# Second attention of a two-layer trunk: part of the output projection made within the last heads' steps, the gate multiplied into its weights

## The chip, the cores and the metric

The kernel runs on one core of one Trainium2 chip. The metric is the device time of one execution in microseconds (us); lower is better. Engines are named as in the profile: PE (TensorE matmul), PEld (its weight loads), DVE (VectorE), ACT (ScalarE), POOL (GpSimd), SP (SyncE); a q behind a name is that engine's queue of transfers.

## The reference

Two layers over 512 latent tokens of 1024 features with 256 context tokens, all in float32. Each layer is a token mixer, a layer norm of the gated sum, and a gated feed-forward with a convolution. The change lies in layer 1, between its mixer (neighbourhood attention) and its feed-forward:

```
y, yc = na_mixer(a_lat, a_ctx, na_w_qkv[slot], na_rpb[slot], na_w_o[slot], need_ctx)
...
h_lat = layer_norm(DEEPNORM_ALPHA * h_lat + g1 * y, ln1_g[i], ln1_b[i])
f = conv_ffn(modulate(h_lat, sh2, sc2), ffn_w_in[i], ffn_conv_w[i], ffn_conv_b[i], ffn_w_out[i])
```

Here `y` is the attention's output `o` (512 tokens by 16 heads of 64) times `w_o` (1024 by 1024), and `g1` is a vector of 1024, one value for each output feature. So `g1 * (o @ w_o)` equals `o @ (w_o * g1)`.

## The kernel before

Every float32 product is three matmuls: each operand is split into a high part (`wh`, `oh`, `axh`: a CAST on ACT) and a low part (`wl`, `ol`, `axl`: raw minus high, on DVE or POOL), and `mm3` (line 132) adds high times high, low times high and high times low in one PSUM bank. Weights come as units of 128 by 2048 (`unit`, line 114): a transfer into one of two `raw` buffers, ACT casts, POOL or DVE subtractions. `unit` can multiply a gate into `raw` first (lines 117 to 119); before, only the last feed-forward's `w_out` did.

Layer 1's attention goes by 32 steps, one for each head and each half of the queries (lines 1156 to 1187). A step makes the scores (`scn`), maxima and exponentials (`sn`, `en`), the reciprocal (DVE, line 1076) and the scaling of `en` (POOL, line 1077), then, for the step before, transposes (`trn`, split into `pt` by ACT and DVE), the product with the values (`pvn`), and its sum into `on` (`otn` on ACT and DVE, then POOL, line 1111). `ORDER1` writes down in which places of a step these come and where extra work (`f0` to `f5`) goes in: other heads' projections, weight units (`n_unit`), and splits of finished parts of `on` (`n_part`). A scheduler of the framework then sets each engine's final order; each engine takes its own instructions strictly in that order.

The output projection has four tiles of 128 tokens. For each, eight chunks `c` of 128 features (two heads each) are multiplied with `w_o` into two banks `yps` of 512 columns: `out_mm` (line 148), six matmuls of 128x512 per chunk and tile, 192 in all. Chunks 0 to 6 of tile 0 and 0 to 3 of tile 1 can be made while the last step is still under way (lines 1171 to 1174); all others follow in `mixer_out` (line 756), which runs after the attention. It loads `xr`, the residual, on ACT's queue into two buffers (line 773; line 748 in the profile), multiplies it by `eg` (DVE, line 775) and adds `eb` (POOL by halves, line 693). When a tile's banks are full, DVE multiplies them by the gate (line 787), adds `xr` (line 792), takes the norm (lines 676 to 686, with `rs` on POOL, line 681); PE transposes `z` (`ltr`, line 703), ACT scales and casts (`ft`, `axh`), POOL or DVE makes `axl` (line 719). `u` (line 814) are the first matmuls of the feed-forward; for its first two units they take 256 tokens at a time, so that they need two tiles.

Of the kernel before, what the change touches and what calls it, by code (L numbers as in the profile page):

```python
# [16 lines left out]
D = 1024  # L17
# [27 lines left out]
def trunk(ctx, tc, x, cx, cc, ada_w, ada_b, vec, ln1_g, ln1_b, ln2_g, ln2_b, w_in, w_out, m_in, m_qb,  # L45
# [44 lines left out]
    sil = const.tile([128, KD, 32], F32, name="sil")  # L90
    nc.vector.memset(sil, 0.0)
    nc.scalar.activation(sil[:, :, 0:2], cct, AF.Silu)
# [44 lines left out]
    def wide(src, xw, eng):  # L137
        raw = load(src)
        nc.scalar.copy(xw[0], raw)
        eng.tensor_tensor(xw[1], raw, f(xw[0]), op=ALU.subtract)  # L140
        return xw
# [6 lines left out]
    def out_mm(pss, part, us, c):  # L148
        wh, wl = us[c // 2]
        for hf in range(2):  # L150
            b = (c % 2) * 1024 + hf * 512
            mm3(pss[hf], *part, wh[:, b:b + 512], wl[:, b:b + 512], c == 0, c == 7)

# [58 lines left out]
    # =================== layer 0: latent attention ===================  # L212
# [58 lines left out]
    # Features come by blocks. Two tiles of tokens keep up with them; of the others a first part of the sum over the  # L271
    # features, up to the block named here, is made between blocks and kept.
# [269 lines left out]
    # what fills in at a step of layer 0's attention (head of a group of four, group of queries), in places 0 to 2  # L542
# [45 lines left out]
    # layer 0's output weights and the first heads' output, split in pieces between the last steps  # L588
# [4 lines left out]
    def late_pieces():  # L593
# [5 lines left out]
        for u in range(4):  # L599
# [9 lines left out]
            if u == 2:  # L609
                # the buffers of the queries that no further head needs  # L610
# [114 lines left out]
    def new_a(slot):  # L725
        # the latent part in two halves of 256 tokens, but whole where its tokens are permuted (slot 1)
# [13 lines left out]
    def by_block(eng, dram_rows, t, sb, store):  # L740
        # rows of a tile of two grid rows lie in DRAM by (block of 8 columns, row, column)
# [14 lines left out]
    def mixer_out(layer, slot, o, w_o, nt, wl=None, us=(), done=(), banks=()):  # L756
# [7 lines left out]
        g1 = [bcast(wl, gates[layer, 0, s:s + 1], f"g1{s}") for s in range(2 if nt > 4 else 1)]  # L764
        e1 = affine(wp, ln2_g[0:1], ln2_b[0:1]) if layer else None
        dst = new_a(slot)
        for t in range(nt):
# [34 lines left out]
    def ffn(layer, a_in, nt, out_slot, groups):  # L802
# [8 lines left out]
        def up(c):  # L811
# [27 lines left out]
            if layer == 0:  # L839
                # latent tokens of a tile of two grid rows go by blocks of 8 columns: (block, row, column)  # L840
# [107 lines left out]
    # =================== layer 1: neighbourhood attention ===================  # L948
# [11 lines left out]
    us, parts, ends = [], {0: [], 1: []}, []  # L960

    def n_unit(u):
        if u < 12:
            nw[u] = unit(n_qkv[u], eng="m" if u < 2 else "p")
        elif u < 15:
            us.append(unit(n_o[u - 12]))
        else:
            us.append(wide(n_o[3], [acp.tile([128, KD * C], F32R, name="ac" + i, tag="ac" + i, bufs=1) for i in "hl"],
                           nc.gpsimd))

    def n_part(t, c0, c1):
        p, tag = (vp, "vn") if c1 <= 4 else (vp, "qs")
        hl = [p.tile([128, 4, 128], F32R, name=tag, tag=tag, bufs=13 if tag == "vn" else 2)[:, :c1 - c0]
              for i in range(2)]
# [126 lines left out]
    def n_out(h, jj):  # L1101
# [7 lines left out]
        for j in range(2):  # L1109
# [6 lines left out]
    # what fills in at a step of layer 1's attention (head of a group of four, half of the queries), in places 0 to 5  # L1116
# [7 lines left out]
             (3, 1): [[], [("bias", 4)], [("v", 3)], [], [], []]}  # L1124

# [28 lines left out]
    for n, cur in enumerate(steps + [None]):  # L1154
        prev = steps[n - 1] if n else None
        fl = [[] for _ in range(6)]
        if cur:
            h, jj = cur
            fl = fills1(h, jj)
            if (h, jj) == (14, 0):  # L1160
                fl[5].append(lambda: n_part(0, 0, 4))
            if (h, jj) == (14, 1):
                fl[5].append(lambda: n_unit(15))
            if (h, jj) == (15, 0):
                fl[5].append(lambda: n_part(0, 4, 7))
                fl[5].append(lambda: n_part(1, 0, 4))
        else:
# [4 lines left out]
            fl[3] += [lambda t=t, c=c: out_mm(pss[t], parts[t][c], us, c) for t, c0, c1 in ((0, 4, 7), (1, 0, 4))  # L1172
# [25 lines left out]
def layout(i):  # L1198
# [39 lines left out]
    us = []  # L1238
# [48 lines left out]
```

## Time and profile before

| | |
|---|---|
| median of 3 runs | 1791.41 us (1791.40 to 1794.37) |
| the profiled execution, as timed | 1791.4 us |
| its span in the trace | 1790.0 us |
| PE busy | 1714.9 us, 96% of the span, 9776 instructions |
| DVE, ACT, POOL busy | 1094.7, 820.9, 841.8 us |
| last `pvn` of the attention | starts 1356.63, takes 0.74 us |
| first `u` of the feed-forward | 1403.18 us |

Times in the trace count from the start of the span. A busy share is an average over stages; what a stage waits for stands in the waits of its engines, and a wait is put down to the instruction that ended it.

### The profile page before, as it was taken

Reading aid. Unit: us, or ns where it says so; the run is one execution under the profiler, and the core shown is the slowest. Engines: PE = TensorE matmul, PEld = TensorE weight load, DVE = VectorE, ACT = ScalarE, POOL = GpSimd, SP = SyncE. Lnnn points to the kernel's source line nnn. Section 1 sums busy time; section 2 is a strip of 40 time slices with the busy share of each in tenths; the row PEclk is TensorE's granted clock in tenths of the full one; section 3 lists DMA queues with packets and bytes.
Section 4 is the critical chain, followed back from the end, with each engine's and each line's share of the span. In section 5 each row is a group of like instructions: output and inputs, shape, how many; then the busy total and the mean of one; then the engine's idle time right before and its main releaser. Section 6 shows DMA issues by size and latency. Waiting matters only on the chain. (4 is left out here: it accounts for less than half of the span.)

```text
span 1790.0 us, 25828 instructions
## 1 busy us (share of the span) xinstructions
PE 1714.9 (96%) x9776; PEld 1463.1 (82%) x9776; DVE 1094.7 (61%) x1971; ACT 820.9 (46%) x1660; POOL 841.8 (47%) x808
## 2 busy tenths in 40 slices
PE   6999999998999999999999989999988899999996
PEld 4877878887888888888888878989977788888885
DVE  4477787775763555555457756766765634444587
ACT  2366666664554233233222266666672553333332
POOL 3224233433452233333227468768783644453464
PEclk8999999999999999999999999999999999999998
DMA  8324354334341222221122212111122432132231
GB/s 309 121 106 177 143 184 171 138 139 138 113 174 48 71 71 71 71 71 51 68 71 71 95 66 91 57 54 57 57 86 82 165 112 100 71 118 94 88 113 59
DMA packets 35845, 185.37 MB, mean 104 GB/s; under 512 B 4072, under 2 KB 6520, under 8 KB 19080
## 3 DMA queue, kind: packets, MB, share of 16 engines
q1 hardware_dynamic: 32552, 173.23, 27.4%
q10 hardware_dynamic: 3168, 10.49, 1.7%
q8 instruction: 77, 1.26, 0.3%
q14 instruction: 48, 0.39, 0.1%
HBM read 174.23 MB, written 9.50 MB: 103 GB/s over the span
## 5 line engine op out<-in xcount | busy, mean ns | idle before, releaser
L129 POOL TENSOR_TENSOR wl<-raw,wh 128x512 fp32r<-128x512 f32 x284 | 381.0, 1374 | 457.3 <-ACT wh L125 457.1
L133 PE MATMUL u<-axh,wh 128*128 128x512 f32 (+1 forms) x736 | 281.6, 383 | 4.4 <-DVE z L787 3.3
L125 ACT CAST wh<-raw 128x512 fp32r<-128x512 f32 x324 | 179.2, 621 | 232.5 <-PE u L134 103.5
L134 PE MATMUL u<-axl,wh 128*128 128x512 f32 (+1 forms) x736 | 281.1, 382 | 0.6 <-POOL axl L719 0.6
L135 PE MATMUL u<-axh,wl 128*128 128x512 f32 (+1 forms) x736 | 281.0, 382 | 0.0
L898 DVE TENSOR_TENSOR acc<-ops,acc 128x512 f32<-128x512 f32 x168 | 114.7, 688 | 175.5 <-PE ops L135 174.9
L133 PE MATMUL ops<-wh,hh 128*128 128x512 f32 x440 | 174.2, 396 | 10.8 <-DVE ut L836 7.0
L134 PE MATMUL ops<-wl,hh 128*128 128x512 f32 x440 | 174.3, 397 | 0.0
L135 PE MATMUL ops<-wh,hl 128*128 128x512 f32 x440 | 172.4, 395 | 0.0
L133 PEld LDWEIGHTS u<-axh,wh 128*128 128x128 f32 x736 | 139.7, 190 | 30.7 <-DVE z L787 3.5
L134 PEld LDWEIGHTS u<-axl,wh 128*128 128x128 f32 x736 | 139.7, 190 | 26.8 <-POOL axl L719 0.9
L135 PEld LDWEIGHTS u<-axh,wl 128*128 128x128 f32 x736 | 139.6, 190 | 26.5
L493 POOL TENSOR_SCALAR e<-e,st 128x768 f32<-128x768 f32 (+1 forms) x96 | 75.1, 783 | 167.8 <-DVE st L492 143.1
L832 ACT ACTIVATE ut<-u,vt 128x512 f32<-128x512 f32 x88 | 68.3, 777 | 185.2 <-DVE ut L836 86.1
L834 DVE SCALAR_TENSOR_TENSOR ut<-u,vt,ut 128x511 f32<-128x511 f32 x88 | 65.7, 746 | 128.3 <-ACT ut L832 128.3
L133 PEld LDWEIGHTS ops<-wh,hh 128*128 128x128 f32 x440 | 83.8, 191 | 28.5 <-issue 7.4
L135 PE MATMUL uc<-ach,wl 128*128 128x256 f32 x352 | 99.6, 283 | 0.0
L134 PE MATMUL uc<-acl,wh 128*128 128x256 f32 x352 | 99.6, 283 | 0.0
L133 PE MATMUL uc<-ach,wh 128*128 128x256 f32 x352 | 99.6, 283 | 0.0
L135 PEld LDWEIGHTS ops<-wh,hl 128*128 128x128 f32 x440 | 83.5, 190 | 18.0
L134 PEld LDWEIGHTS ops<-wl,hh 128*128 128x128 f32 x440 | 83.8, 190 | 15.3
L511 DVE TENSOR_TENSOR pl<-ptr,ph 128x512 fp32r<-128x512 f32 x112 | 76.3, 687 | 19.8 <-ACT ph L507 18.3
(480 smaller groups left out, 4367.9 us busy)
## 6 DMA issues: line engine op xcount, KB each, us to landing
raw<-w_in SPq DMA_DIRECT2D x44, 1024.0 KB
raw<-ada_w SPq DMA_DIRECT2D x40, 1024.0 KB
raw<-w_out SPq DMA_DIRECT2D x22, 1024.0 KB
raw<-n_qkv SPq DMA_DIRECT2D x12, 1024.0 KB
rr<-resid ACTq DMA_DIRECT2D x10, 512.0 KB
raw<-ada SPq DMA_DIRECT2D x4, 1024.0 KB
ar<-ada SPq DMA_DIRECT2D x8, 512.0 KB
raw<-m_o SPq DMA_DIRECT2D x4, 1024.0 KB
```

The lines of the kernel that those rows point to most:

```text
L125: nc.scalar.copy(hi[:, a:b], raw[:, a:b])
L129: e.tensor_tensor(lo[:, a:b], raw[:, a:b], f(hi[:, a:b]), op=ALU.subtract)
L133: nc.tensor.matmul(ps, ah, bh, start=start, stop=False)
L134: nc.tensor.matmul(ps, ah, bl, start=False, stop=False)
L135: nc.tensor.matmul(ps, al, bh, start=False, stop=stop)
L493: done["p"] = nc.gpsimd.tensor_scalar(e[:, :n], e[:, :n], st[:, 2:3], 1.0, op0=ALU.mult, op1=ALU.mult).ins
L511: nc.vector.tensor_tensor(pl, tr, f(ph), op=ALU.subtract)
L832: nc.scalar.activation(u, p, AF.Identity, bias=cb[:, i:i + 1], scale=cw[:, 3 * i + 1:3 * i + 2])
L834: nc.vector.scalar_tensor_tensor(u[:, 1:], p[:, :n - 1], cw[:, 3 * i:3 * i + 1], u[:, 1:], op0=ALU.mult, op1=ALU.add)
L898: nc.vector.tensor_tensor(a[:, sl], ps, a[:, sl], op=ALU.add)
```

## The change

1. `n_half` makes chunks 0 to 3 (heads 0 to 7) of tiles 1, 2 and 3 in a bank of its own, `yp`: 12 matmuls for each of three tiles and two halves, 72 in all. ACT copies the bank to `zp` in SBUF. A table, `LAST1`, puts these and the splits they need into the steps of heads 13 to 15.
2. In `mixer_out` POOL adds `zp` to `xr` for these tiles (six instructions of 128x512). The banks then take only chunks 4 to 7 of tiles 1 to 3; those of tile 1, but for the last, are made in the last step.
3. The gate is multiplied into the four units of `w_o` on DVE (four instructions of 128x512 each), and its vector is loaded at the start of layer 1. The eight multiplies of the banks (line 787) go; `z` is `xr` plus the bank.
4. For room, `sil` goes to another pool and the scratch space of the framework's dynamic transfers is set to 512.

```diff
-    def wide(src, xw, eng):
+    def wide(src, xw, eng, gate=None):
         raw = load(src)
+        for a in range(0, 2048 if gate is not None else 0, 512):
+            nc.vector.tensor_tensor(raw[:, a:a + 512], raw[:, a:a + 512], gate[:, a % D:a % D + 512], op=ALU.mult)
...
-    def out_mm(pss, part, us, c):
+    def out_mm(pss, part, us, c, first=0, stop=7, halves=(0, 1)):
         wh, wl = us[c // 2]
-        for hf in range(2):
+        for hf in halves:
             b = (c % 2) * 1024 + hf * 512
-            mm3(pss[hf], *part, wh[:, b:b + 512], wl[:, b:b + 512], c == 0, c == 7)
+            mm3(pss[hf], *part, wh[:, b:b + 512], wl[:, b:b + 512], c == first, c == stop)
...
                 by_halves(nc.gpsimd, xt, xt, e1[1], ALU.add)
+                if firsts[t]:
+                    by_halves(nc.gpsimd, xt, xt, zp[:, t - 1], ALU.add)
...
             for hf in range(2):
                 hs = slice(hf * 512, hf * 512 + 512)
                 ps = pss[hf]
-                nc.vector.tensor_tensor(z[:, hs], ps, g1[s][:, hs], op=ALU.mult)
                 if layer == 0:
+                    nc.vector.tensor_tensor(z[:, hs], ps, g1[s][:, hs], op=ALU.mult)
...
                 else:
-                    nc.vector.tensor_tensor(z[:, hs], xt[:, hs], z[:, hs], op=ALU.add)
+                    nc.vector.tensor_tensor(z[:, hs], xt[:, hs], ps, op=ALU.add)
...
+    g1t = bcast(p5, gates[1, 0, 0:1], "g1t")
+    zp = p5.tile([128, 3, D], F32, name="zp")
...
-            us.append(unit(n_o[u - 12]))
+            us.append(unit(n_o[u - 12], gate=g1t))
...
+    def n_half(t, hf):
+        ps = bank("yp", [128, 512])
+        for c in range(4):
+            out_mm([ps, ps], parts[t][c], us, c, 0, 3, (hf,))
+        nc.scalar.copy(zp[:, t - 1, hf * 512:hf * 512 + 512], ps)
...
+    LAST1 = {(13, 0): [(5, "part", (1, 0, 4))],
+             (13, 1): [(1, "half", (1, 0)), (4, "half", (1, 1)), (5, "part", (2, 0, 4))],
+             (14, 0): [(1, "half", (2, 0)), (5, "part", (3, 0, 4))],
+             (14, 1): [(1, "half", (2, 1)), (5, "unit", (15,))],
+             (15, 0): [(1, "half", (3, 0)), (5, "part", (0, 0, 4)), (5, "part", (0, 4, 7, "qs"))],
+             (15, 1): [(1, "half", (3, 1)), (5, "part", (1, 4, 7))]}
...
-            fl[3] += [lambda t=t, c=c: out_mm(pss[t], parts[t][c], us, c) for t, c0, c1 in ((0, 4, 7), (1, 0, 4))
+            fl[3] += [lambda t=t, c=c: out_mm(pss[t], parts[t][c], us, c, 4 * t) for t, c0, c1 in ((0, 4, 7), (1, 4, 7))
                       for c in range(c0, c1)]
...
-        a4 = mixer_out(1, 2, o, n_o, 4, wl, us, [7, 4], pss)
+        a4 = mixer_out(1, 2, o, n_o, 4, wl, us, [7, 7, 4, 4], pss, (0, 4, 4, 4), zp)
```

How this moves instructions is told by each engine's order, in which the new file's lines are some 2 to 12 higher. First DVE in the attention, where the third unit of `w_o` comes in. Line 1076 is the reciprocal before (1088 now), line 986 (998) the split of a value tile, and ISA the maximum with the bias. Before:

```order
L986 TENSOR_TENSOR vn<-vps,vn 128x4x64
L1063 TENSOR_REDUCE sn<-scn 128x1
L1076 RECIPROCAL sn<-sn 128x1
L1064 ISA scn,sn<-scn,bm_12935,sn 128x256
L1064 ISA sn 128x1
L1076 RECIPROCAL sn<-sn 128x1
L1066 TENSOR_SCALAR sn<-sn 128x1
L1091 TENSOR_TENSOR pt<-trn,pt 128x4x128
```

And now:

```order
L998 TENSOR_TENSOR vn<-vps,vn 128x4x64
L1075 TENSOR_REDUCE sn<-scn 128x1
L1088 RECIPROCAL sn<-sn 128x1
L116 TENSOR_TENSOR raw<-raw,bc_g1t 128x512
L1076 ISA scn,sn<-scn,bm_12938,sn 128x256
L1076 ISA sn 128x1
L116 TENSOR_TENSOR raw<-raw,bc_g1t 128x512 x3
L1088 RECIPROCAL sn<-sn 128x1
L1103 TENSOR_TENSOR pt<-trn,pt 128x4x128
```

Four multiplies of the weights now stand between one reciprocal and the next, which had only the maximum between them.

Second, DVE after the attention: from the first multiply of `xr` on. Before:

```order
L775 TENSOR_TENSOR xr<-xr,bc_eg 128x1024
L792 TENSOR_TENSOR z<-xr,z 128x512 x2
L676 BN_STATS bn<-z 128x6 x2
L787 TENSOR_TENSOR z<-yps,bc_g_13787 128x512 x2
L678 BN_AGGR mv<-bn 128x2
L792 TENSOR_TENSOR z<-xr,z 128x512 x2
L145 TENSOR_TENSOR ol<-on,oh 128x1024
L680 TENSOR_SCALAR rs<-mv 128x1
L775 TENSOR_TENSOR xr<-xr,bc_eg 128x1024
L676 BN_STATS bn<-z 128x6 x2
L686 TENSOR_SCALAR z<-z,mv,rs 128x1024
```

Now (the first row is the multiply for tile 1, as it is above):

```order
L777 TENSOR_TENSOR xr<-xr,bc_eg 128x1024
L796 TENSOR_TENSOR z<-xr,yps 128x512
L144 TENSOR_TENSOR ol<-on,oh 128x512
...
L680 BN_AGGR mv<-bn 128x2
L682 TENSOR_SCALAR rs<-mv 128x1
L796 TENSOR_TENSOR z<-xr,yps 128x512
L678 BN_STATS bn<-z 128x6
L777 TENSOR_TENSOR xr<-xr,bc_eg 128x1024
L796 TENSOR_TENSOR z<-xr,yps 128x512
L688 TENSOR_SCALAR z<-z,mv,rs 128x1024
```

The multiply of `xr` for tile 2 stood behind both halves of tile 1's `z`; now it stands between them, and ahead of the norm of tile 0 as before.

Third, POOL after the attention. Before:

```order
L693 TENSOR_TENSOR xr<-xr,bc_eb 128x512 x4
L681 TENSOR_TENSOR rs<-rs,mhalf 128x1
L693 TENSOR_TENSOR xr<-xr,bc_eb 128x512 x4
L681 TENSOR_TENSOR rs<-rs,mhalf 128x1
L719 TENSOR_TENSOR axl<-ft,axh 128x4x128
L129 TENSOR_TENSOR wl<-raw,wh 128x512
```

Now:

```order
L695 TENSOR_TENSOR xr<-xr,bc_eb 128x512 x4
L695 TENSOR_TENSOR xr<-xr,zp 128x512 x2
L683 TENSOR_TENSOR rs<-rs,mhalf 128x1
L695 TENSOR_TENSOR xr<-xr,bc_eb 128x512 x2
L695 TENSOR_TENSOR xr<-xr,zp 128x512
...
L695 TENSOR_TENSOR xr<-xr,bc_eb 128x512 x2
L126 TENSOR_TENSOR wl<-raw,wh 128x512
L695 TENSOR_TENSOR xr<-xr,zp 128x512
L126 TENSOR_TENSOR wl<-raw,wh 128x512
L695 TENSOR_TENSOR xr<-xr,zp 128x512
L683 TENSOR_TENSOR rs<-rs,mhalf 128x1
L721 TENSOR_TENSOR axl<-ft,axh 128x4x128 x4
```

The six additions of `zp` and two weight splits stand ahead of the third `rs` and of the first `axl`, which stood behind the second `rs`.

## Rows read from the trace of the kernel before

**Rows 1.** Windows: us, busy time (instructions) of each engine, granted PE clock, transfers.

```profile
1254.00:1318.00 64.00, 63.46 (x449) 59.11 (x448) 45.94 (x127) 42.40 (x90) 50.70 (x68) 1.00 0.19 59
1318.00:1335.70 17.70, 13.10 (x87) 11.52 (x85) 13.22 (x45) 13.53 (x27) 17.45 (x19) 0.90 0.35 120
1335.70:1357.40 21.70, 21.11 (x116) 18.00 (x114) 7.59 (x16) 7.71 (x15) 7.06 (x13) 1.00 0.06 25
1357.40:1403.20 45.80, 35.17 (x152) 28.01 (x152) 33.34 (x43) 18.40 (x41) 26.69 (x22) 0.93 0.38 120
...
1286.00:1293.00 7.00, 7.00 (x62) 7.00 (x61) 6.12 (x20) 4.41 (x11) 6.09 (x10) 1.00 0.46 152
```

**Rows 2.** Waits of PE, 1318 to 1358: us in total, times, longest.

```profile
PE pvn L1098 <- DVE pt L1091: 2.4, 3, 1.2
```

**Rows 3.** Waits of PE, 1358 to 1411.

```profile
PE ltr L703 <- DVE z L686: 3.6, 2, 2.1
PE u L133 <- DVE z L787: 3.3, 1, 3.3
```

**Rows 4.** Timeline of PE, last pvn and first u: start, duration, instruction [idle before].

```profile
1356.63 0.74 PE L1098 MATMUL pvn<-pt,vn 128*128 128x256 f32 x4 [0.56 <-DVE pt L1091]
...
1404.34 0.58 PE L134 MATMUL u<-axl,wh 128*128 128x256 f32 x1 [0.57 <-POOL axl L719]
```

**Rows 5.** Timeline of PE: matmuls of the projection in the tail.

```profile
1385.71 0.39 PE L133 MATMUL yps<-wh,oh 128*128 128x512 f32 x1
...
1389.14 0.40 PE L133 MATMUL yps<-wh,oh 128*128 128x512 f32 x1
```

**Rows 6.** Line 693, adding eb on POOL: ns min/median/max, first and last start.

```profile
L693 POOL TENSOR_TENSOR xr<-xr,bc_eb x8: 1262/1493/2150, 1368.3 to 1388.0; 128x512 f32<-128x512 f32 x8
```

**Rows 7.** Groups of instructions, 1357.40 to 1403.20: busy us, mean ns | idle before.

```profile
L792 DVE TENSOR_TENSOR z<-xr,z 128x512 f32<-128x512 f32 x7 | 6.7, 986 | 0.0
...
L787 DVE TENSOR_TENSOR z<-yps,bc_g 128x512 f32<-128x512 f32 x8 | 5.1, 678 | 0.7 <-PE yps L135 0.7
...
L719 POOL TENSOR_TENSOR axl<-ft,axh 128x512 fp32r<-128x512 f32 x3 | 4.3, 1432 | 0.0
```

**Rows 8.** Line 119, gate multiply in the last feed-forward: ns min/median/max; then mean.

```profile
L119 DVE TENSOR_TENSOR raw<-raw,bc_g x8: 677/1564/1782, 1714.9 to 1745.1; 128x512 f32<-128x512 f32 x8
...
L119 DVE TENSOR_TENSOR raw<-raw,bc_g 128x512 f32<-128x512 f32 x8 | 10.5, 1360 | 1.5 <-DMA raw<-w_out 1.5
```

**Rows 9.** Timeline of DVE: two reciprocals where the third unit comes in.

```profile
1291.60 0.15 DVE L1076 RECIPROCAL sn<-sn 128x1 f32<-128x1 f32 x1
...
1292.23 0.16 DVE L1076 RECIPROCAL sn<-sn 128x1 f32<-128x1 f32 x1
```

**Rows 10.** Waits of PE, 1230 to 1318.

```profile
PE kp L133 <- DVE kk L1019: 0.3, 1, 0.3
```

**Rows 11.** Timeline of DVE in the tail: xr and z.

```profile
1370.93 1.88 DVE L775 TENSOR_TENSOR xr<-xr,bc_eg 128x1024 f32<-128x1024 f32 x1 [1.61 <-DMA xr<-resid]
1372.73 2.38 DVE L792 TENSOR_TENSOR z<-xr,z 128x512 f32<-128x512 f32 x2
...
1381.26 1.23 DVE L775 TENSOR_TENSOR xr<-xr,bc_eg 128x1024 f32<-128x1024 f32 x1 [1.30 <-DMA xr<-resid]
...
1385.00 1.64 DVE L775 TENSOR_TENSOR xr<-xr,bc_eg 128x1024 f32<-128x1024 f32 x1 [0.57 <-DMA xr<-resid]
```

**Rows 12.** Timeline of ACT's queue: transfers of xr for tiles 2 and 3.

```profile
1375.13 1.20 ACTq L748 DMA_DIRECT2D xr<-resid  x2
...
1378.79 1.19 ACTq L748 DMA_DIRECT2D xr<-resid  x2
```

**Rows 13.** Timeline of POOL in the tail: eb for tiles 1 and 3, rs.

```profile
1372.88 3.38 POOL L693 TENSOR_TENSOR xr<-xr,bc_eb 128x512 f32<-128x512 f32 x2 [1.16 <-DVE xr L775]
...
1386.78 2.56 POOL L693 TENSOR_TENSOR xr<-xr,bc_eb 128x512 f32<-128x512 f32 x2 [1.22 <-DVE mv L678]
...
1395.76 0.94 POOL L681 TENSOR_TENSOR rs<-rs,mhalf 128x1 f32<-128x1 f32 x1 [2.96 <-DVE rs L680]
```

More of the change, by code (lines that the diff above doesn't have):

```diff
@@ L89, in trunk @@
     make_identity(nc, ident)
-    sil = const.tile([128, KD, 32], F32, name="sil")
-    nc.vector.memset(sil, 0.0)
-    nc.scalar.activation(sil[:, :, 0:2], cct, AF.Silu)
     mhalf = const.tile([128, 1], F32, name="mhalf")
@@ L220, in trunk @@
     adap, close_ada = pool("adap", side="right")
+    sil = adap.tile([128, KD, 32], F32, name="sil")
+    nc.vector.memset(sil, 0.0)
+    nc.scalar.activation(sil[:, :, 0:2], cct, AF.Silu)
     pw, close_pw = pool("pw", side="right")
@@ L754, in affine, with mixer_out @@
         return eg, eb
-    def mixer_out(layer, slot, o, w_o, nt, wl=None, us=(), done=(), banks=()):
+    def mixer_out(layer, slot, o, w_o, nt, wl=None, us=(), done=(), banks=(), firsts=(0,) * 6, zp=None):
         wp, close_wp = pool(f"wo{layer}", side="right" if layer else "left")
@@ L763, in mixer_out @@
             us.append(wide(w_o[3], xw, nc.vector))
-        g1 = [bcast(wl, gates[layer, 0, s:s + 1], f"g1{s}") for s in range(2 if nt > 4 else 1)]
+        g1 = [bcast(wl, gates[layer, 0, s:s + 1], f"g1{s}") for s in range(2 if layer == 0 else 0)]
         e1 = affine(wp, ln2_g[0:1], ln2_b[0:1]) if layer else None
@@ L782, in mixer_out @@
             for c in range(c0, 8):
-                out_mm(pss, part[c - c0], us, c)
+                out_mm(pss, part[c - c0], us, c, firsts[t])
             for hf in range(2):
@@ L958, in trunk @@
     vb, nw, qsc, kks, qq, bms, sx, px, pvn = {}, {}, {}, {}, {}, {}, {}, {}, {}
-    us, parts, ends = [], {0: [], 1: []}, []
+    us, parts, ends = [], {t: {} for t in range(4)}, []
+    g1t = bcast(p5, gates[1, 0, 0:1], "g1t")
+    zp = p5.tile([128, 3, D], F32, name="zp")
     def n_unit(u):
@@ L965, in n_unit, with n_part @@
         elif u < 15:
-            us.append(unit(n_o[u - 12]))
+            us.append(unit(n_o[u - 12], gate=g1t))
         else:
             us.append(wide(n_o[3], [acp.tile([128, KD * C], F32R, name="ac" + i, tag="ac" + i, bufs=1) for i in "hl"],
[L969 to L973, printed above, removed]
+                           nc.gpsimd, g1t))
+    def n_part(t, c0, c1, tag="vn"):
+        hl = [vp.tile([128, 4, 128], F32R, name=tag, tag=tag, bufs=13 if tag == "vn" else 2)[:, :c1 - c0]
               for i in range(2)]
-        parts[t] += split_rows(o, c0, c1, slice(t * 128, t * 128 + 128), *hl, nc.gpsimd)
+        parts[t] |= dict(zip(range(c0, c1), split_rows(o, c0, c1, slice(t * 128, t * 128 + 128), *hl, nc.gpsimd)))
+    def n_half(t, hf):
[3 more added lines that the diff above has]
+        nc.scalar.copy(zp[:, t - 1, hf * 512:hf * 512 + 512], ps)
     def n_v(g, t):
@@ L1159, in trunk @@
             fl = fills1(h, jj)
[L1160 to L1166, printed above, removed]
+            for i, fn, args in LAST1.get((h, jj), ()):
+                fl[i].append(lambda fn=fn, args=args: {"part": n_part, "half": n_half, "unit": n_unit}[fn](*args))
         else:
@@ L1278 @@
     arrays = layout(inputs)
-    nc = bacc.Bacc("TRN2", target_bir_lowering=False, num_devices=1)
+    nc = bacc.Bacc("TRN2", target_bir_lowering=False, num_devices=1, dynamic_dma_scratch_size=512)
     args = [nc.dram_tensor(n, arrays[n].shape, mybir.dt.from_np(arrays[n].dtype), kind="ExternalInput").ap()
```

## Prediction, made before the changed kernel ran

> **What bounds the kernel now.** I read the table of windows first, because 96% of the span is TensorE and only a stretch with idle PE has anything to give. Up to 1318 PE is full: 63.46 of 64.00 us [rows 1]. From 1318 to 1357.40, the last steps of the attention, it is busy 13.10 of 17.70 and 21.11 of 21.70 us, so 5.2 us are idle, and over the first of these stretches the granted clock is 0.90: a fifth of 17.70 us, 3.5 us, at the lower level (1.2 GHz) in place of 2.4, which costs 1.8 us. From 1357.40 to 1403.20, the tail (output projection, normalisation, first feed-forward matmuls), PE is busy 35.17 of 45.80 us [rows 1].
>
> Then the waits of PE, for who ends them: of the 5.2 us idle in the last steps 2.4 end with the split of the transposed probabilities [rows 2]; in the tail 3.6 us on the norm of z and 3.3 on a bank that DVE frees with z [rows 3]. None is a wait for matmuls: the tail is set by a chain of xr (a transfer, a multiply on DVE, adds on POOL), z, norm, transpose, axl, u. Call E the end of the last pvn, 1356.63 + 0.74 = 1357.37. The first u that can go on starts at 1404.34, E + 47.0, and it had waited for POOL's axl [rows 4]. From there PE is full again.
>
> **Matmuls that move.** 192 matmuls of 128x512 make the projection in both versions; none is saved. Before E stood 66 (tile 0: 7 pairs of heads, tile 1: 4, six each); now 132 (72 into yp, 42 of tile 0, 18 of tile 1). So 66 more come before E. Start to start at the higher clock, from 1385.71 to 1389.14, 15 of them take 3.43 us, 0.229 each [rows 5]: 66 x 0.229 = 15.1 us. They can fill what PE idles there, 5.2 us, and keep the clock up, 1.8 us. E therefore moves by 15.1 - 7.0 = 8.1 us at least and by 15.1 at most. I take 10: the last waits for pt [rows 2] belong to the closing steps, which the order of the last pvn keeps, so about 5 us are filled.
>
> **Six copies on ACT** (yp to zp, 128x512): ACT is busy 7.71 of 21.70 us there [rows 1]; nothing. The three more splits on POOL (128x512, 1.26 to 1.49 us by an instruction of that size [rows 6]) stand between steps in which POOL idles, 7.06 busy of 21.70 from 1335.7 on [rows 1]; but from 1318 to 1335.7 it is busy 17.45 of 17.70, and a split that lands there delays the chain by its own length. At most 3 x 1.49 = 4.5 us, at least 0; the yp matmuls are what PE does meanwhile, so I take 0 within the 10. The gate's vector stays one transfer, issued a whole attention ahead of its first use, and the moves for room shift no instruction of these stretches: nothing.
>
> **The gate in the weights.** 16 multiplies of 128x512 on DVE are added, all ahead of E, and 8 of 0.678 us (z<-yps,bc_g, 5.4 us together) leave the tail [rows 7]. The same instruction stands later in this program, in the last feed-forward: 8 times, 677 ns at its shortest, 1564 in the median, 1360 in the mean [rows 8]. 16 x 1.36 = 21.8 us. The order puts blocks of four ahead of RECIPROCALs, as for the third unit of the weights in the order shown above, so the chain reciprocal, en on POOL, transpose, pvn is held by up to 4 x 1.36 = 5.4 us at each of the four blocks. In the trace those two reciprocals start 0.6 us apart [rows 9]. What hides it is PE's own projection work: from 1230 to 1318 PE's longest wait is 0.3 us [rows 10], so there is a cover, but of a depth that no row tells. Bounds 0 (all covered) and 10 us (the second rival). I take 3, nearer to the lower end, since PE has 63.46 of 64.00 us of other work in that stretch.
>
> What the pair 677 and 1564 ns shows is one instruction with two durations [rows 8], and z<-xr,z likewise has a mean of 986 in the tail [rows 7]. The Trainium skill says why (SBUF — State Buffer, section "SBUF: two separate sides"): a DVE operation with two SBUF inputs and a GpSimd operation take the shared port pair as an exclusive lock for the whole instruction. By that rule a gate block, two SBUF inputs beside a POOL that is busy 79% of the stretch, comes out near the long value, 16 x 1.56 = 25 us, and the new z<-xr,yps with one input in PSUM near the short one. The sum here uses the mean.
>
> **The tail after.** 60 matmuls stay behind E (6 + 6 + 24 + 24) where 126 stood, 15.1 us less work for PE. Does u start sooner? I follow the chain with the rows' own durations, as offsets from E.
> - xr of tile 1 lands at 13.6 (DVE waited for it); DVE multiplies it until 15.4 [rows 11], POOL adds eb until 18.9 [rows 13].
> - New: POOL then adds zp for tile 1, two at the 1.49 to 1.69 of its neighbours [rows 6, 13], until 22.2. z of tile 1 waits for it.
> - z of tile 0 is done at 17.7, as before, and frees its xr [rows 11]: the transfer of xr for tile 2 is issued [rows 12], lands 6.1 us later at 23.9, its multiply ends at 25.1. In the new order this multiply stands ahead of the second half of z of tile 1, and of the norm of tile 0: both wait for the transfer. So z of tile 1 ends at 26.4 (half of the 2.38 behind 25.1), and only then is xr for tile 3 issued, where it was at 21.4 before. Plus 6.2 and 1.64 [rows 11]: 34.2.
> - POOL: eb 2.6 (36.8), then wl, zp, wl, zp at 1.49 each (42.8) and rs 0.9 (43.7) [rows 6, 13]. Behind this rs stand axl: three of 1.43 until both tiles of the first half have one, 48.0 [rows 7].
>
> So u goes on at E + 48.0 in place of 47.0: +1. The bounds: with POOL at its shortest, 1.26 in place of 1.49 to 1.69 [rows 6, 13], some 13 instructions of that chain save 4 us, -3; with a transfer for tile 3 as long as that for tile 1, 13.6 less the time to its issue just after E in place of 6.2, some 6 more, +7, but that one shared the transfer engines with three others, so I take +5. DVE's 5.4 us of gate multiplies lie beside this chain and take nothing off it.
>
> **The sum.** The profiled execution is 1790.0 us of span and 1791.4 us as timed, 1.4 us around it, and equal to the median of the runs. 1791.4 + 10 + 3 + 1 = 1805.4 us, slower by 0.8%. The matmuls leave a stretch that does not wait for them and go to one that is nearly full. Ends of the sum: 8.1 + 0 - 3 gives 1796.5, 15.1 + 3 + 5 gives 1814.5.
>
> **Rivals.**
> 1. *The tail is set by its matmuls* (faster). If u starts when PE is through, 66 x 0.229 = 15.1 us go. With the gates covered (0) and E at +10: 1791.4 + 10 - 15.1 = 1786.3. For it: PE is busy 77% of the tail, the norm is released by z, z by yps. Against it: the u at E + 47.0 waited for POOL [rows 4], DVE waited for three of the xr shown [rows 11], and their two buffers remain. It decides from the point where POOL is through with tile 3 before E + 33. Chance 0.12.
> 2. *DVE becomes the bound of the attention* (slower still). 12 of the 16 multiplies fall in 1254 to 1318 by the order; 45.94 + 12 x 1.36 = 62.3 of 64.00 us. The fullest stretch of DVE in the rows is 6.12 of 7.00 us, 87% [rows 1]; at that share 62.3 takes 71.6, +7.6, and the first block, some 9 us ahead of that stretch, about 2 more. 1791.4 + 10 + 9.6 + 1 = 1812.0. Against: PE's other work. Chance 0.22.
> 3. *Half of the matmuls' time comes back*: E + 10, gates covered, tail -7.5 because POOL's short durations and the earlier weight splits (four wl now stand before E on DVE) shorten the chain: 1793.9, no change that can be told. Chance 0.08.
> That the matmuls might not move at all is excluded: in PE's order the six groups of yp stand among the steps, ahead of the last pvn.
>
> **How the numbers follow.** The forecast has 0.58, with 1796.5 to 1814.5. Below 1794 lie rival 1 and about half of rival 3; above 1818 only the far end of rival 2. So 1794 to 1818. A measurement of this kernel tells 0.2%, 3.6 us, from no change: faster 0.12, same 0.08, slower 0.80.
>
> **What would show it.** Right: the last pvn ends 11 to 16 us later than at 1357.4; the first u after it comes 46 to 51 us behind; PE's waits in the tail grow by about 15 us, on z and axl; xr of tile 3 is multiplied some 33 us behind E; raw<-raw,bc_g1t has a mean over 1 us. Wrong: a u within 40 us of E (rival 1), an E later by 18 us or more with DVE named in waits before 1330 (rival 2), or an E under 8 us later, which would mean that PE had more hidden idle time than its rows show.

## The result, and the profile after

The changed kernel takes 1804.09 us in the median of 4 runs (1802.17 to 1806.49), the kernel before 1792.03 us (4 runs): a ratio of 1.0064 with a 95% interval of 1.0051 to 1.0076, slower by 12 us. Forecast were 1805.4 us and a range of 1794 to 1818.

I cut both traces at the same four events: the first `qp` after 1232 us (the projection of the last heads' queries begins), the last `kp`, the end E of the last `pvn`, the first `u` that uses `axl`. In the profiled execution after (span 1804.7 us, 14.7 more than before) they stand at 1237.81, 1325.64, 1372.72 and 1420.64; before at 1234.23, 1317.85, 1357.37 and 1404.34. (The last cut is at the first `u` with `axl` because single `u` stand ahead of it, each followed by a wait: before, one at 1399.55 and one at 1403.18, so 1403.18 is not the first.) E and the first `u` with `axl` after:

```profile
1371.62 1.10 PE L1110 MATMUL pvn<-pt,vn 128*128 128x256 f32 x8
...
1420.64 0.58 PE L131 MATMUL u<-axl,wh 128*128 128x256 f32 x1 [0.38 <-POOL axl L721]
```

| stretch | before | after | difference | forecast |
|---|---|---|---|---|
| up to the first `qp` | 1234.2 | 1237.8 | +3.6 | 0 |
| first `qp` to last `kp`: the gate's multiplies | 83.6 | 87.8 | +4.2 | +3 |
| last `kp` to E: the early groups | 39.5 | 47.1 | +7.6 | +10 |
| E to the first `u` with `axl`: the tail | 47.0 | 47.9 | +0.9 | +1 |
| from that `u` to the end | 385.7 | 384.1 | -1.6 | 0 |

Little of the first line can be laid to the change. Five other kernels, which share the moves for room and, up to that `qp`, have the same order of instructions on PE, ACT and POOL, stand between -0.8 and +1.3 there (table below). The lag of 3.6 us arises mainly in three places: 1.4 us by 19 us into the span, 1.5 us at 1021 and 0.8 us at 1056. At 1021 PE has just come back from idle (3.0 us of it in both traces), and the 512-column matmuls start 0.43 us apart, by the timeline, until about 1020.8 before and 1025.3 after, then 0.23; the granted clock is 0.85 from 1020 to 1023 before and 0.52 from 1021 to 1025.5 after. This lag is also why the profiled execution is further above before (14.7 us of span) than the medians are (12.1).

PE by stretch after, from the table of windows (the last `kp` to E in two pieces, then the tail):

```profile
1325.70:1343.40 17.70, 17.06 (x108) 14.93 (x108) 12.97 (x43) 12.98 (x27) 17.70 (x18) 1.00 0.33 120
1343.40:1372.72 29.32, 29.32 (x160) 25.03 (x158) 15.88 (x25) 16.65 (x34) 19.02 (x24) 1.00 0.21 72
1372.72:1419.50 46.78, 21.93 (x85) 16.50 (x85) 26.78 (x38) 12.45 (x29) 30.05 (x26) 0.76 0.39 116
```

Against [rows 1]: the last steps went from 34.21 busy of 39.40 us at a clock of 0.90 and 1.00 to 46.38 of 47.02 at 1.00. E itself, with the lines above it in the table, is 15.4 us later. Nearly all idle time there is used up (0.6 us is left), and the stretch is as long as its matmuls. The tail kept its length, but PE is busy 21.93 of 46.78 us where it was 35.17 of 45.80, and the granted clock fell from 0.93 to 0.76: what was taken out of it has become idle time. Waits of PE ahead of the last `kp`, and in the tail:

```profile
PE trn L1094 <- DVE sn L1078: 1.3, 1, 1.3
PE vps L130 <- DVE kk L1031: 0.9, 1, 0.9
PE kp L130 <- DVE kk L1031: 0.3, 1, 0.3
```

```profile
PE yps L130 <- DVE z L796: 11.7, 2, 10.4
PE u L130 <- ACT axh L719: 3.6, 1, 3.6
PE u L130 <- DVE z L796: 3.6, 1, 3.6
```

The first three are what of the gate shows in PE's waits: before, only the last of them was there [rows 10]. In all, PE's idle time from `qp` to `kp` grew from 0.5 to 3.2 us and its busy time from 83.1 to 84.6. Matched matmul by matmul, the lag grows by 1.7 us at 1254 to 1256 and by 2.4 at 1302 to 1306, behind the first and the third block of multiplies; the second and the fourth block delay PE by 0.1 us or less. The next three are the 15 us of matmuls: PE now waits 10.4 us at once for a bank of tile 0 that `z` has not yet emptied. The chain of the tail itself, DVE and then POOL, is the forecast one nearly to the microsecond:

```profile
1397.37 1.22 DVE L777 TENSOR_TENSOR xr<-xr,bc_eg 128x1024 f32<-128x1024 f32 x1 [4.10 <-DMA xr<-resid]
1398.51 0.68 DVE L796 TENSOR_TENSOR z<-xr,yps 128x512 f32<-128x512 f32 x1
...
1405.85 1.23 DVE L777 TENSOR_TENSOR xr<-xr,bc_eg 128x1024 f32<-128x1024 f32 x1 [4.31 <-DMA xr<-resid]
```

```profile
1407.15 3.46 POOL L695 TENSOR_TENSOR xr<-xr,bc_eb 128x512 f32<-128x512 f32 x2 [2.47 <-DVE xr L777]
1410.58 1.25 POOL L126 TENSOR_TENSOR wl<-raw,wh 128x512 fp32r<-128x512 f32 x1
1411.80 1.71 POOL L695 TENSOR_TENSOR xr<-xr,zp 128x512 f32<-128x512 f32 x1
...
1414.69 1.26 POOL L695 TENSOR_TENSOR xr<-xr,zp 128x512 f32<-128x512 f32 x1
1415.91 0.55 POOL L683 TENSOR_TENSOR rs<-rs,mhalf 128x1 f32<-128x1 f32 x1
1416.43 5.41 POOL L721 TENSOR_TENSOR axl<-ft,axh 128x512 fp32r<-128x512 f32 x4
```

`xr` of tile 3 is multiplied at E + 33.1 (forecast some 33), `rs` stands at E + 43.2 (forecast 42.8), and `u` at E + 47.9 (forecast 48.0).

### The profile page after: what moved, and what is told of

It is laid out like the page before. It is cut to its first block, busy times and chain, and to the rows that moved or that the text cites. A ratio compares the mean times of both kernels' runs of the same rounds, so it can differ in the third digit from the quotient of the medians.

```text
span 1804.7 us, 25847 instructions
## 1 busy us (share of the span) xinstructions
PE 1718.0 (95%) x9776; PEld 1463.5 (81%) x9776; DVE 1100.6 (61%) x1979; ACT 825.3 (46%) x1669; POOL 855.4 (47%) x817
## 5 line engine op out<-in xcount | busy, mean ns | idle before, releaser
L130 PEld LDWEIGHTS u<-axh,wh 128*128 128x128 f32 x736 | 139.4, 190 | 33.6 <-DVE z L796 3.9
L130 PEld LDWEIGHTS ops<-wh,hh 128*128 128x128 f32 x440 | 84.1, 191 | 28.7 <-issue 7.2
```

Of the source, the lines that this page charges most:

```text
L130: nc.tensor.matmul(ps, ah, bh, start=start, stop=False)
```

## The experiments

All times are medians; a ratio is to the kernel before on the same chip, with its 95% interval. The stretches are cut as above in each kernel's profiled execution, except that the last is from E to the first `ops` (the feed-forward's first down projection), since a late tile 3 shows only there. "At qp" is the lag to before at the first `qp`. What follows `ops` is 346.5 to 347.7 us in all of them.

| kernel | time | ratio (interval) | at qp | qp to kp | kp to E | E to u | E to ops |
|---|---|---|---|---|---|---|---|
| before | 1792.03 | 1 | 0 | 83.6 | 39.5 | 47.0 | 85.5 |
| after | 1804.09 | 1.0064 (1.0051 to 1.0076) | +3.6 | 87.8 | 47.1 | 47.9 | 84.4 |
| gate_only | 1796.52 | 1.0021 (1.0012 to 1.0030) | +1.2 | 88.1 | 40.6 | 44.7 | 82.4 |
| half_only | 1803.08 | 1.0062 (1.0049 to 1.0074) | -0.8 | 83.6 | 46.9 | 53.8 | 89.2 |
| pad_tail | 1808.55 | 1.0090 (1.0076 to 1.0104) | +1.3 | 88.1 | 47.1 | 45.9 | 88.7 |
| xr4_after | 1805.91 | 1.0078 (1.0064 to 1.0092) | +1.2 | 87.8 | 47.1 | 50.2 | 87.1 |
| zp_dve | 1805.41 | 1.0070 (1.0054 to 1.0085) | +0.9 | 89.1 | 47.6 | 46.7 | 85.4 |
| aff_before | 1796.55 | 1.0022 (1.0013 to 1.0030) | +9.9 | 83.6 | 39.1 | 38.2 | 81.4 |
| aff_half | 1795.28 | 1.0019 (1.0010 to 1.0027) | +9.4 | 83.6 | 46.9 | 33.6 | 72.2 |
| aff_after | 1807.35 | 1.0083 (1.0070 to 1.0097) | +9.4 | 88.0 | 46.9 | 42.4 | 78.3 |
| early_before | 1795.11 | 1.0009 (1.0000 to 1.0018) | +10.6 | 83.6 | 39.7 | 36.7 | 77.7 |
| early_half | 1795.86 | 1.0015 (1.0006 to 1.0024) | +13.1 | 83.6 | 46.9 | 33.2 | 71.7 |
| early_after | 1805.11 | 1.0068 (1.0054 to 1.0082) | +8.1 | 87.9 | 47.0 | 39.5 | 76.1 |
| late_before | 1795.92 | 1.0022 (1.0012 to 1.0033) | +9.2 | 83.6 | 39.1 | 40.8 | 82.8 |

**Each half of the change alone.** half_only takes the gate out of the weights again; gate_only is the kernel before with the gate in the weights and nothing else (and the two moves for room).

```diff
 # half_only, against after
-            us.append(unit(n_o[u - 12], gate=g1t))
+            us.append(unit(n_o[u - 12]))
...
-        nc.scalar.copy(zp[:, t - 1, hf * 512:hf * 512 + 512], ps)
+        hs = slice(hf * 512, hf * 512 + 512)
+        nc.vector.tensor_tensor(zp[:, t - 1, hs], ps, g1t[:, hs], op=ALU.mult)
...
-                    nc.vector.tensor_tensor(z[:, hs], xt[:, hs], ps, op=ALU.add)
+                    nc.vector.tensor_tensor(z[:, hs], ps, gate[:, hs], op=ALU.mult)
+                    nc.vector.tensor_tensor(z[:, hs], xt[:, hs], z[:, hs], op=ALU.add)
```

```diff
 # gate_only, against before
-            us.append(unit(n_o[u - 12]))
+            us.append(unit(n_o[u - 12], gate=g1t))
...
-                nc.vector.tensor_tensor(z[:, hs], ps, g1[s][:, hs], op=ALU.mult)
...
-                    nc.vector.tensor_tensor(z[:, hs], xt[:, hs], z[:, hs], op=ALU.add)
+                    nc.vector.tensor_tensor(z[:, hs], xt[:, hs], ps, op=ALU.add)
```

> The six groups of early matmuls and zp stay, the gate is not multiplied into the weights: DVE multiplies each yp bank by it on the way to zp (6 instructions) and the banks of the tail as before (8). My theory, by the trace of the changed kernel: the 16 multiplies delay the attention by 4.3 us (lag to the kernel before grows from 3.5 to 7.8 us between 1230 and 1326), so this kernel takes 1800 us, and its reciprocals near 1265 and 1300 stand no longer behind multiplies. Rival (gates hidden, the whole cost is the moved matmuls): 1804, no change to the changed kernel.

> The kernel before with nothing but the gate in the weights (and the moves for room). My theory: the attention ends some 4 us later, the tail loses 8 multiplies of DVE that lie beside its chain, so 1795 to 1796, slower than before by 3 to 4 us. Rival (the multiplies are hidden, the tail gains its 5.4 us of DVE): 1787 to 1792.

In the attention the two costs stand apart: every kernel with the gate in its weights takes 87.8 to 89.1 us from `qp` to `kp`, every one without 83.6; every kernel with the early groups takes 46.9 to 47.6 from `kp` to E, every one without 39.1 to 40.6. From `qp` to E the gate alone costs 5.6 us (gate_only) and the groups alone 7.4 (half_only); together they cost 11.8, 1.2 less than their sum. gate_only's waits of PE name the same two places as after's:

```profile
PE trn L1086 <- DVE sn L1070: 1.4, 1, 1.4
PE vps L130 <- DVE kk L1023: 0.9, 1, 0.9
```

The totals are another matter. gate_only gets 3.1 us back by `ops`: its tail lost eight multiplies of DVE, which I had said take nothing off. The net is 4.5 + 1.1 - 3.1 = 2.5 us, and the medians show 4.7 (the ratio's interval is 0.12 to 0.30%, 2 to 5 us): some 2 us lie outside these stretches or within the noise. The time is near the one I expected, but by two larger terms, 5.6 and -3.1, in place of 4 and nothing. And half_only did not come to 1800: its attention did what I expected, but its tail is 4.8 us longer than after's by `ops`, and 5.9 by `u`. DVE in that tail:

```profile
1393.77 3.43 DVE L126 TENSOR_TENSOR wl<-raw,wh 128x512 fp32r<-128x512 f32 x2
1397.12 0.68 DVE L678 BATCH_NORM_STATS2 bn<-z 128x6 f32<-128x512 f32 x1
...
1398.52 2.11 DVE L777 TENSOR_TENSOR xr<-xr,bc_eg 128x1024 f32<-128x1024 f32 x1 [0.28 <-DMA xr<-resid]
1400.55 1.27 DVE L796 TENSOR_TENSOR z<-yps,bc_g1t 128x512 f32<-128x512 f32 x2
1401.75 2.73 DVE L797 TENSOR_TENSOR z<-xr,z 128x512 f32<-128x512 f32 x2
...
1411.07 1.29 DVE L796 TENSOR_TENSOR z<-yps,bc_g1t 128x512 f32<-128x512 f32 x2 [3.88 <-DMA resid<-z]
```

In after the same statistics of tile 1 come 5.5 us sooner, at E + 27.7 in place of E + 33.2, and the weight splits stand behind them:

```profile
1400.42 0.68 DVE L678 BATCH_NORM_STATS2 bn<-z 128x6 f32<-128x512 f32 x1
```

So some 3.4 of the 5.9 us to `u` are the order, which here puts two weight splits of 3.43 us ahead of tile 1's statistics. The multiplies that are back stand in the way later on: those of tile 2 stand ahead of tile 1's scaling by the norm (line 688, at 1405.01), and those of tile 3 wait 3.88 us for the store of an earlier `z`. The gate in the weights thus goes with a tail shorter by 4.8 us and costs 4.2 us in the attention. In the full change it is about neutral (the ratios are 1.0062 without and 1.0064 with it), and the groups alone, 7.4 us ahead of E and a tail 3.7 us longer than before's, cost as much as the whole change. How much of the tail's difference is the length of the multiplies themselves is not shown. The expected 1800 was wrong by this.

**Is the tail set by matmuls?** pad_tail makes 24 matmuls of each of tiles 2 and 3 twice.

```diff
+            for c in range(c0, 8) if layer and t >= 2 else ():
+                out_mm(pss, part[c - c0], us, c, firsts[t])
             for c in range(c0, 8):
                 out_mm(pss, part[c - c0], us, c, firsts[t])
```

> The changed kernel with 48 matmuls of 128x512 more in the tail: chunks 4 to 7 of tiles 2 and 3 are made twice into the same banks, the second pass counts. 48 x 0.229 = 11 us of PE work at the higher clock are put back where 15 were taken out. My theory (the tail is set by transfer, POOL and DVE, not by matmuls): within 2 us of the changed kernel, 1802 to 1806. Rival (the tail is set by its matmuls): 1815.

Neither number came. 11 us of matmuls cost 4.5 us in the median. `u` did not come later (E + 45.9 against 47.9), as the first theory has it: for the first half of the features there is room for all of them. But the last `yps` went from E + 32.9 to E + 45.6, so tile 3's transposes came at 1431.16, E + 60.5 in place of 53.6, and `ops` 4.3 us later:

```profile
1416.26 0.39 PE L132 MATMUL yps<-ach,ol 128*128 128x512 f32 x1
1431.16 1.06 PE L705 MATMUL ltr<-ident,z 128*128 128x128 f32 x8
```

The tail has two ends: the first `u` wait for tiles 0 and 1, and the next for tiles 2 and 3. My chain ended at the first.

**Which part of the chain holds it?** xr4_after gives `xr` four buffers; zp_dve lets DVE add `zp`.

```diff
-            xt = wp.tile([128, D], F32, name="xr", tag="xr", bufs=2)
+            xt = wp.tile([128, D], F32, name="xr", tag="xr", bufs=4 if layer else 2)
```

```diff
-                if firsts[t]:
-                    by_halves(nc.gpsimd, xt, xt, zp[:, t - 1], ALU.add)
...
+                    if firsts[t]:
+                        nc.vector.tensor_tensor(z[:, hs], zp[:, t - 1, hs], ps, op=ALU.add)
+                        nc.vector.tensor_tensor(z[:, hs], xt[:, hs], z[:, hs], op=ALU.add)
```

> The changed kernel with four buffers for xr in place of two, so that all four transfers are issued right after the attention's end. My theory: the chain loses the wait for the transfers of tiles 2 and 3 (DVE waited 4.1 and 4.3 us for them), xr of tile 3 is multiplied 10 us sooner, and u starts some 6 to 10 us sooner, so 1795 to 1798; what then ends last is POOL, with 14 additions of 1.3 to 1.7 us ahead of the third rs. Rival (POOL alone sets the tail): 1802 to 1804.

> The changed kernel with zp added by DVE (to the bank, then xr), not by POOL to xr: six additions of 1.25 to 1.7 us, 8 us, leave POOL and six of 0.7 to 1.3 us come to DVE. Theory A (POOL's additions are what keeps the tail long: the third rs stood behind all of them at E + 43.2): u comes 4 to 7 us sooner, 1797 to 1800. Theory B (the order in which the scheduler puts DVE's work behind transfers and weight splits sets it, whoever adds): 1802 to 1806.

Neither helped (1805.91, above both numbers named for it, and 1805.41). In xr4_after the waits for transfers are gone (0.27 and 0.18 us where after has 4.10 and 4.31), tile 3's `xr` is multiplied at E + 20.5, 12.6 us sooner, and `u` comes 2.3 us later:

```profile
1387.44 1.93 DVE L777 TENSOR_TENSOR xr<-xr,bc_eg 128x1024 f32<-128x1024 f32 x1 [0.27 <-DMA xr<-resid]
1390.74 2.06 DVE L777 TENSOR_TENSOR xr<-xr,bc_eg 128x1024 f32<-128x1024 f32 x1 [0.18 <-DMA xr<-resid]
```

```profile
1395.14 2.55 POOL L695 TENSOR_TENSOR xr<-xr,bc_eb 128x512 f32<-128x512 f32 x2
1397.64 1.29 POOL L695 TENSOR_TENSOR xr<-xr,zp 128x512 f32<-128x512 f32 x1
1398.89 0.55 POOL L683 TENSOR_TENSOR rs<-rs,mhalf 128x1 f32<-128x1 f32 x1
```

POOL now takes eleven additions, those of tiles 2 and 3 among them, before the first `rs`, which stands at E + 28.7 and stood at E + 20.3. The `u` itself waits for the third `axl`, and on POOL two scalings of the feed-forward's vectors and another `rs` now stand ahead of that one:

```profile
1414.35 1.37 POOL L754 TENSOR_SCALAR bc_eg<-bc_eg 128x1024 f32<-128x1024 f32 x1
1415.80 2.08 POOL L755 TENSOR_SCALAR bc_eb<-bc_eb 128x1024 f32<-128x1024 f32 x1
...
1418.47 5.31 POOL L721 TENSOR_TENSOR axl<-ft,axh 128x512 fp32r<-128x512 f32 x3
```

In zp_dve POOL is free of six additions, yet `u` comes only 1.2 us sooner and `ops` 1.0 us later: the third `axl` still stands behind the `rs` of tile 2, and that waits for DVE, whose `z` of tile 2 stands behind two weight splits.

```profile
1404.76 3.43 DVE L126 TENSOR_TENSOR wl<-raw,wh 128x512 fp32r<-128x512 f32 x2
...
1416.57 0.55 POOL L683 TENSOR_TENSOR rs<-rs,mhalf 128x1 f32<-128x1 f32 x1 [4.35 <-DVE rs L682]
```

So theory B holds for zp_dve, in its range (1805.4) and in what the trace shows: when the wait for transfers or POOL's additions go, another chain of nearly the same length is left, and the scheduler's order decides which. I had priced one of them.

**Taking the work on xr out of the tail.** aff_before, aff_half and aff_after (before, half_only, after) apply `eg` and `eb` once, where layer 0 stores the residual; `xr` gets four buffers.

```diff
+            if last and not final:
+                for t in range(4):
+                    a = acc[:, t]
+                    nc.vector.tensor_tensor(a, a, e2[0][0], op=ALU.mult)
+                    by_halves(nc.gpsimd, a, a, e2[0][1], ALU.add)
+                    nc.scalar.dma_start(resid[1, t * 128:t * 128 + 128], a)
...
-                nc.vector.tensor_tensor(xt, xt, e1[0], op=ALU.mult)
-                by_halves(nc.gpsimd, xt, xt, e1[1], ALU.add)
```

> The kernel before with the residual's scale and shift (eg, eb) applied once where layer 0 stores it, so that the tail has no multiply on DVE, no eb on POOL, and four buffers for xr. Theory A (the tail is set by what must be done to xr, not by matmuls): the tail falls to its matmuls, u starts some 5 to 8 us sooner; the multiplies in layer 0 cost 0 to 3; 1784 to 1789. Theory C (the tail is long for other reasons: the norm chain, the weight splits): 1790 to 1795.

> The same edit on the kernel with the early groups but no gate in the weights. Theory A: the attention ends 4.3 us sooner than in the version with the gate, the tail has 14 short DVE multiplies that no longer stand in a chain with xr: 1785 to 1790, the fastest or as fast as the kernel before with this edit. If the gate multiplies were hidden: as the version with the gate.

> The same edit on the changed kernel; POOL keeps only the six additions of zp, which can run before the banks are full. Theory A: its tail has 60 matmuls, 15 us less PE work than before, so u starts at E + 30 to 36 in place of 48 and the time is 1788 to 1793; the moved matmuls then pay in the tail what they cost ahead of it. Theory C: 1800 or more.

Theory A's time came in none of the three (1796.55, 1795.28 and 1807.35; only the last lies where theory C had it). The tail did what theory A says in aff_before. It is 38.2 us there, 8.8 shorter, with PE busy 34.53 of them, and what is left of PE's waits up to 1420 us is the start and one cast:

```profile
1366.82:1405.06 38.24, 34.53 (x153) 28.36 (x152) 24.81 (x36) 17.19 (x38) 12.70 (x12) 0.91 0.30 106
```

```profile
PE yps L133 <- ACT oh L144: 3.7, 1, 3.7
PE u L133 <- ACT axh L717: 1.9, 1, 1.9
```

In such a tail the groups pay back their price: from E to `ops` aff_half has 72.2 us against 81.4, 9.2 less, for 7.8 more ahead of E. That is a draw, and so are the medians (1795.28 and 1796.55, intervals that overlap). It isn't the 15 us of the moved matmuls, for without them the tail no longer hangs on its matmuls: PE is busy 20.11 of 33.55 us, at a granted clock of 0.78.

```profile
1374.10:1407.65 33.55, 20.11 (x78) 14.97 (x78) 26.45 (x40) 12.35 (x29) 18.62 (x17) 0.78 0.45 143
```

aff_after's tail has 42.4 because of the order again: ACT's `ft` stood 8.66 us behind the issue of a feed-forward transfer on ACT's own queue, which by the profile waited for POOL:

```profile
1406.55 0.32 ACTq L863 DMA_DIRECT2D rr<-resid  x1
1406.91 1.15 ACT L708 ACTIVATE ft<-ltr,comb 128x128 f32<-128x128 f32 x3 [8.66 <-POOL bc_eb L755]
```

```profile
PE ltr L705 <- ACT ft L708: 8.8, 2, 8.5
```

The price at layer 0's end was 10 us, not 0 to 3: PE waited 7.2 us there for norms that stood behind the new multiplies on DVE.

```profile
PE ltr L703 <- DVE acc L686: 7.2, 2, 5.3
```

**The same without touching layer 0.** early_before, early_half and early_after load, scale, shift and store each tile of the residual from the attention's steps; late_before (no groups, no gate) keeps tiles 0 and 1 in SBUF and should scale them in the last two steps.

```diff
+    def n_resid(t):
+        if not e1:
+            e1.extend((bc5(ln2_g[0:1], "eg"), bc5(ln2_b[0:1], "eb")))
+        xt = p5.tile([128, D], F32, name="xe", tag="xe", bufs=1)
+        nc.sync.dma_start(xt, resid[1, t * 128:t * 128 + 128])
+        nc.vector.tensor_tensor(xt, xt, e1[0], op=ALU.mult)
+        by_halves(nc.gpsimd, xt, xt, e1[1], ALU.add)
+        nc.sync.dma_start(resid[1, t * 128:t * 128 + 128], xt)
...
+            if h in (4, 5, 6, 7) and jj == 1:
+                fl[5].append(lambda t=h - 4: n_resid(t))
```

```diff
+        for t in range(2):
+            xs.append(p5.tile([128, D], F32, name=f"xs{t}"))
+            by_block(nc.sync, resid[1], t, xs[t], False)
...
+        with tc.issue_after(ends[0]):
+            nc.vector.tensor_tensor(xs[t], xs[t], e1[0], op=ALU.mult)
+            by_halves(nc.gpsimd, xs[t], xs[t], e1[1], ALU.add)
...
+            if h == 15:
+                fl[5].append(lambda t=jj: n_resid(t))
```

> The kernel before with the residual's scale and shift applied during the attention (one tile in each of the steps of heads 4 to 7: a load, one multiply on DVE, two additions on POOL, a store in place), so that layer 0's end is untouched and the tail has neither; four buffers for xr. From the version that did it at layer 0's end: that end took 9 us longer, the tail was 8.7 us shorter (u at E + 38.2, 66 more matmuls of the projection behind E than in the changed kernel). Theory: no loss at layer 0's end, 0 to 2 us in the attention, tail at E + 38: 1783 to 1785. Rival (four more multiplies and eight additions cost in the attention what 16 multiplies did, 4 us and more): 1788 to 1792.

> The same on the kernel with the early groups and no gate in the weights. From its version with the edit at layer 0's end: E 7.4 us later than without the groups, u at E + 33.6, 4.7 us nearer than 38.2. Theory: the groups cost 7.4 and give back 4.7 even in a tail that is set by matmuls, so 1786 to 1788, 3 us above the kernel before with this edit. Rival (the groups pay once nothing else holds the tail): 1780 or less.

> The same on the changed kernel. E 4.3 us later for the gate and 7.4 for the groups. In its version with the edit at layer 0's end ACT stood 8.7 us behind a transfer of the feed-forward's residual that waited for POOL; the order here has that transfer elsewhere. Theory: u at E + 34 to 36, 1790 to 1793. Rival (the order hurts again): 1797 to 1800.

> The kernel before with the residual of tiles 0 and 1 loaded early in the attention into two buffers of their own, multiplied and shifted within the two steps of head 15 (DVE busy 7.6 and POOL 7.1 of 21.7 us there), no early groups, no gate in the weights; tiles 2 and 3 use the two xr buffers from the attention's end on; the feed-forward's residual transfers are held behind the last features. Nothing is moved into the stretch in which the same work cost 10 us. Theory (tail set by what must be done to xr): lag 0 until the last steps, E at most 1 to 2 us later, u at E + 37 to 39 in place of 47: 1783 to 1787, faster than both kernels. Rival (multiply and additions in the last steps delay the attention's end by as much, or the weight splits hold u): 1790 or more.

None of these theories' times came either: each lies 8 to 12 us below the measured one. The rival's 1790 or more came for late_before, but its loss lies elsewhere: 8 us stand far ahead of E, and `u` is only 1.8 us later than the theory had it. All four shorten the tail (36.7, 33.2, 39.5 and 40.8 us to `u`), and all four lose 8 to 11 us in one place, 1080 to 1120 us, far ahead of the steps into which I had written the work: the scheduler had moved the loads and multiplies to the first heads. In late_before one instruction shows it. DVE took the multiply of `xs` before its transfer had landed, and PE waited behind DVE:

```profile
1085.39 1.23 DVE L977 TENSOR_TENSOR xs<-xs,bc_eg 128x1024 f32<-128x1024 f32 x1 [5.99 <-DMA xs<-resid]
```

```profile
PE vps L130 <- DVE kk L1037: 5.9, 1, 5.9
```

Its four additions on POOL stayed in the last steps (1358.6 to 1366.8), and there they cost nothing ahead of E: `kp` to E is 39.1 us.

early_before has the lowest ratio of all variants and is within the noise of before (1.0000 to 1.0018). Without its loss its tail would be worth 7.8 us by `ops`; a version that keeps the one and avoids the other was not run. The groups do not pay here either: early_half has 6.0 us less from E to `ops` than early_before, for 7.2 more ahead of E.

## Why the prediction was right

- *E moves by at least 8.1 us, I take 10.* Measured 7.6 from the last `kp` to E, and 7.4 in half_only against before: the lower bound was nearly the value, too high by half a microsecond. I took 10 because I held back 2 us for waits on `pt` in the closing steps; PE is busy 46.38 of 47.02 us there, and no such wait is left. That the matmuls fill what PE idles and keep the clock at 1.00 was right.
- *The gate: 16 x 1.36 = 21.8 us on DVE, bounds 0 and 10, I take 3.* Measured 4.2 in the stretch, 5.6 in gate_only by E; two of the four blocks delay PE and two don't. The mean duration was wrong, and the forecast had named it as a sign: 0.91 us, not over 1 (the 16 take 14.6 us in the timeline).

```profile
L116 DVE TENSOR_TENSOR raw<-raw,bc_g1t x12: 671/958/1539, 1248.4 to 1300.6; 128x512 f32<-128x512 f32 x12
...
L137 DVE TENSOR_TENSOR raw<-raw,bc_g1t x4: 679/889/1217, 1321.4 to 1324.2; 128x512 f32<-128x512 f32 x4
```

  The rule of the Trainium skill that I had set beside it (SBUF — State Buffer, "SBUF: two separate sides") would have made it 16 x 1.56 = 25 us, and the trace does not agree with that use of it: the lengths run from 671 to 1539 ns, and POOL's busy share does not tell how many of the instructions get a long one. Seven of the 16 took 671 to 703 ns, and three of these overlap no POOL instruction in the trace; the nine that took 870 ns or more all overlap one. The other half of that use came: the eight `z<-xr,yps`, with one input in PSUM, all took the short length.

```profile
L796 DVE TENSOR_TENSOR z<-xr,yps x8: 665/684/690, 1387.6 to 1416.0; 128x512 f32<-128x512 f32 x8
```

- *5.4 us of DVE work that leave the tail take nothing off it.* Wrong, and hidden by the total: gate_only's tail is 3.1 us shorter by `ops`, and half_only's, with these multiplies back and six more ahead of E, is 4.8 us longer than after's, in part by the order that comes with them. The term of the tail came out right all the same because I had followed the changed kernel's own order.
- *The tail does not get shorter, +1.* Measured +0.9 to `u`, on the path that I had written down, with `xr` of tile 3 and the third `rs` where I put them. Right for this kernel; but the chain is not the only one that long, as xr4_after and zp_dve show, and the stretch from `u` to the end (-1.6; the transposes of tile 3 stand at E + 53.6 in place of 55.5) was not in the sum.
- *Rival 1, the tail is set by its matmuls*: it did not come, PE's waits in the tail grew as the forecast said. Its condition alone is not enough: in aff_half POOL is through with `xr` of tile 3 at E + 20, `u` stands at E + 33.6, and the groups give back 9.2 us by `ops`, about what they cost, but not the 15.1 of the rival.
- *Rival 2, DVE bounds the attention*: no; the multiplies were too short for it, and PE is idle 3.2 us in all from `qp` to `kp`.

So the sum of 14 was made of terms that were too high by 2.4 (groups), too low by 1.2 (gate) and too high by 1.7 (E to the end, +1 forecast, 0.9 - 1.6 measured). What is left, 11.1 us, is the profiled execution's difference from the first `qp` on; the medians moved by 12.1, and the bounds of the sum, 1796.5 to 1814.5, held them. That the forecast lies only 1.3 us above the median is partly luck: its errors had different signs, and part of the 12.1 us is in no stretch that it priced.

## What to carry to other kernels

Matmuls that leave a stretch which waits for something else save next to nothing there, and cost their full length less the idle time of where they go: read both from the windows, busy against length, before moving them. When a chain of small operations holds a stretch, look for the second chain beside it; here, as far as xr4_after and zp_dve show, chains of nearly the same length stood side by side, and only taking away their common cause (the work on `xr`) showed the bound of the matmuls, in the kernel that still had them in its tail. An operation without a dependency on the step into which it is written can be moved far ahead by the scheduler, as here to the first heads, and there it can wait for a transfer with everything else of its engine behind it.

## What I had not expected

- The price of the early groups is the same, 46.9 to 47.6 us from `kp` to E, in nine kernels with quite different neighbours: a stretch that PE fills is a stable measure. The tails, which PE does not fill, went from 33 to 54 us to `u`, much of it by the order that a small edit brings with it.
- Four multiplies on DVE and eight additions on POOL cost some 10 us at layer 0's end and, with their loads and stores, 8 to 11 in the first heads; two multiplies and their loads go with a loss of 8 there (late_before), and 16 multiplies on DVE 4.2 in the later heads. What such work costs was set here by what stood behind it in its queue, not by its length.
- The span up to the same `qp` differs by 4.4 us between kernels that have the same order up to there on PE, ACT and POOL (-0.8 to +3.6); part of it is where the granted clock rises again after the same idle stretch.
